# A first activation sum on VectorE, and an output projection with the norms' gains folded into its weights

## The chip, the cores and the metric

The kernel runs on one core of a Trainium2 chip. The metric is the device time of one execution in microseconds (us), as the median of several runs. TensorE (PE) multiplies, VectorE (DVE), ScalarE (ACT) and GpSimd (POOL) work elementwise, and each engine executes its own list of instructions strictly in the order in which the program gave them. Transfers are started by SyncE (SP) and by ScalarE.

## The reference

One layer of a streaming encoder runs over 2048 prompt frames and 64 decode frames, all in float32. D_MODEL is 1024 and D_FF is 2816.

```python
def _merge(attn_o, cmlp_o, norm_attn_g, norm_cmlp_g, w_out):
    cat = jnp.concatenate([_rmsnorm(attn_o, norm_attn_g), _rmsnorm(cmlp_o, norm_cmlp_g)], -1)
    return cat @ w_out

def _post(x, mix, ln1_g, ln1_b, w_gate_up, w_down, ln2_g, ln2_b):
    h = _layernorm(ALPHA * x + mix, ln1_g, ln1_b)
    gu = h @ w_gate_up
    f = (jax.nn.silu(gu[..., :D_FF]) * gu[..., D_FF:]) @ w_down
    return _layernorm(ALPHA * h + f, ln2_g, ln2_b)
```

Ahead of `_merge` stand an input projection, a windowed attention and a gated mixer, which the change does not touch. `_rmsnorm` multiplies each of the 1024 features with a gain of its own, after a scale per row.

## The kernel before

**Exact products from two halves.** A float32 matrix product is made of three fast ones. Each operand is split into hi (ScalarE rounds it to a shorter type) and lo (what is left: source minus hi), and `mm3` adds hi·hi, hi·lo and lo·hi in one PSUM bank. The function `split` does both steps: ScalarE's copy at L112, then the subtraction at L113, on VectorE unless GpSimd is named.

**Output projection and first layer norm (`m2_...`).** The 2112 rows lie in 17 tiles of 128 (tile 16 has 64), taken in the order TSEQ (tiles 0 to 3, 16, then 4 to 15). In what follows a tile's number is its place in TSEQ. A tile passes through these steps:

- `m2_load` brings the concatenated mixers (features by rows, `cat_d`) and the residual x into one buffer `catx`.
- `m2_split` multiplies each of the eight feature blocks by its gain column (`vecT`) and splits it: eight ScalarE instructions (L618) and eight on VectorE (L619) write `cathl`.
- `m2_mm` multiplies with half n of the output columns: 24 matmuls into two PSUM banks `po`, one for the attention features and one for the mixer's.
- `m2_add` scales the residual by ALPHA on ScalarE (L633), adds the attention's bank times its row scale (L634) and then the mixer's bank (L635), both on VectorE.
- `m2_ln` takes mean and variance with `bn_stats` and `bn_aggr` (L642, L644), the inverse root on GpSimd (L92), the gain (L648) and the shift (L649).
- `m2_T` transposes on TensorE (L677), copies to SBUF on ScalarE (L679), and ScalarE issues the stores to `h_d` (L683) and `hy_d` (L684).

A loop over t writes these steps out in a fixed order. For t from 5 to 11 it is: add tile t, multiply tile t+1, norm tile t, split tile t+2, transpose tile t-1, load tile t+3; from t = 6 on a few steps follow that prepare the next stage (`hf`). In that steady part the buffers go round so that `cathl` of tile t+2 lies where `catx` of tile t-2 was, so its first write waits for that tile's store to `hy_d`. The six PSUM banks of the ring "x" hold `po`: the second half of a tile's product needs the banks that the first half of the preceding tile's `m2_add` gives back.

**Feed-forward.** The rows are in four blocks b. Products with the gate and up weights are made by Strassen's scheme, seven `product`s per group i of 128 hidden columns. For blocks 1 to 3 the down projection is Strassen's too, over pairs c of two groups (`strassen`). There are 23 such pairs. From the activations g of a pair, four sums (5, 7, 6 and 3) are made by `f_sums` on GpSimd (L879). `put_hi` (ScalarE, L886) and `put_lo` (VectorE, L890) split a sum, and `unit` multiplies a form's half with its weights (three matmuls, L1333 to L1335) and adds the result to y (L1338). All of this is tied to places p0+q in the list `order` of products. p0 is the place of the pair's last product, whose activation completes the pair. Form 5 is put at p0+3 (hi) and p0+4 (lo), and its first unit stands at p0+5.

Of the kernel before, what the change touches and what calls it, by code (L numbers as in the profile page):

```python
# [8 lines left out]
F32 = mybir.dt.float32  # L9
# [36 lines left out]
def hybrid_step(ctx: ExitStack, tc: tile.TileContext, x_prompt, x_sample, xT_prompt, xT_sample, cache_kT, cache_v, w_in,  # L46
# [541 lines left out]
    def split_wo(hf, n, js):  # L588
        if js[0] == 0:
            wo_hl[hf, n] = [wp.tile([P, 4, 512], F32R, name=f"wo{hf}{n}{s}", tag="W") for s in "hl"]  # L590
        hi, lo = wo_hl[hf, n]
        for j in js:
            split(hi[:, j], lo[:, j], wo_raw.pop((hf, n, j)), nc.gpsimd if j > 1 else None)
            wo[n, 4 * hf + j] = (hi[:, j], lo[:, j])

    cat_t, xr_t, po_t = {}, {}, {}

    def of_f1(name, dt, prod):

# [9 lines left out]
    def m2_split(t, ks=range(KD)):  # L609
        m = rows(t)  # L610
        s = cat_t[t][:, 0].rearrange("p (k q) -> p k q", q=P)
        if ks[0] == 0:
            xr_t[t] = (of_f1("cathl", F32R, 2).rearrange("p (s k q) -> p s k q", s=2, q=P) if t == 3 else
                       wp.tile([P, 2, KD, P], F32R, name="cathl", tag="W"))
        c = xr_t[t]
        for k in ks:
            gcol = vecT[:, 8 + k:9 + k]
            nc.scalar.activation(c[:, 0, k, :m], s[:, k, :m], AF.Copy, scale=gcol)  # L618
            nc.vector.scalar_tensor_tensor(out=c[:, 1, k, :m], in0=s[:, k, :m], scalar=gcol,  # L619
                                           in1=c[:, 0, k, :m].bitcast(F32), op0=ALU.mult, op1=ALU.subtract)  # L620

    def m2_mm(t, n):
        m = rows(t)
# [5 lines left out]
    def m2_add(t, n):  # L629
        m = rows(t)  # L630
        ts_ = cat_t[t][:m, 1, n * 512:(n + 1) * 512]
        po = po_t.pop((t, n))
        nc.scalar.activation(ts_, ts_, AF.Copy, scale=ALPHA)  # L633
        nc.vector.scalar_tensor_tensor(out=ts_, in0=po[0][:m], scalar=rstd_a[:m, t:t + 1], in1=ts_, op0=ALU.mult, op1=ALU.add)  # L634
        nc.vector.tensor_tensor(out=ts_, in0=po[1][:m], in1=ts_, op=ALU.add)  # L635

    def m2_ln(t):
        m = rows(t)
        tt = cat_t[t][:, 1]
        st = const.tile([P, 2, 6], F32, name="hst", tag="hst", bufs=2)  # L640
        for n in range(2):
            nc.vector.bn_stats(st[:m, n], tt[:m, n * 512:(n + 1) * 512])  # L642
        mv = const.tile([P, 2], F32, name="hmv", tag="hmv", bufs=2)
        nc.vector.bn_aggr(mv[:m], st[:m])  # L644
        rs = const.tile([P, 1], F32, name="hrs", tag="hrs", bufs=2)
        rstd(rs[:m], mv[:m, 1:2], m, const)

        nc.vector.scalar_tensor_tensor(out=tt[:m], in0=tt[:m], scalar=mv[:m, 0:1], in1=gb_t[0][:m], op0=ALU.subtract, op1=ALU.mult)  # L648
        nc.vector.scalar_tensor_tensor(out=tt[:m], in0=tt[:m], scalar=rs[:m], in1=gb_t[1][:m], op0=ALU.mult, op1=ALU.add)  # L649

    gb_t = {}
# [219 lines left out]
        f = ffs[b, c, prod] = half_form()  # L871
        split(f[:, 0], f[:, 1], src)

    def f_sums(b, c):

        x, y = g_t.pop((b, 2 * c)), g_t.pop((b, 2 * c + 1))
        for prod, o, a, d, op in ((5, y[:, 1], x[:, 1], y[:, 1], ALU.add), (7, x[:, 1], x[:, 0], x[:, 1], ALU.subtract),
                                  (6, x[:, 0], y[:, 1], x[:, 0], ALU.subtract), (3, y[:, 0], y[:, 0], x[:, 0], ALU.subtract)):
            nc.gpsimd.tensor_tensor(out=o, in0=a, in1=d, op=op)  # L879
        for prod, o in ((5, y[:, 1]), (6, x[:, 0]), (7, x[:, 1]), (3, y[:, 0])):  # L880
            f_sum[b, c, prod] = o

    def put_hi(b, c, prod):

# [12 lines left out]
    def product(b, i, prod):  # L897
        n = TB[b] // 2
        w, h = wf.pop((b, i, prod)), forms[b, prod]
        bk = {1: "A", 6: "A", 7: "A", 4: "A", 2: "B", 5: "C", 3: "C"}[prod]  # L900
        new = prod in (1, 2, 5)
        if new:
            acc[i, bk] = (bank({"A": f"A{i % 2}", "C": f"C{i % 2}", "B": "S1"}[bk]) if b else
                          ps1.tile([P, 512], F32, name=f"acc{bk}", tag="x", bufs=6))
        ps = acc[i, bk][:, :n]
        for k in range(4):
            wh, wl, hh, hl = w[:, 0, k], w[:, 1, k], h[:, 0, k, :n], h[:, 1, k, :n]

            nc.tensor.matmul(ps, wh, hh, start=(new and k == 0), stop=False, skip_group_check=not new)  # L909
            nc.tensor.matmul(ps, wh, hl, start=False, stop=False, skip_group_check=not new)  # L910
            nc.tensor.matmul(ps, wl, hh, start=False, stop=(k == 3), skip_group_check=not new)  # L911

        def keep(key):
            part[i, key] = tmp(key)
            nc.scalar.copy(part[i, key][:, :n], ps)  # L915

        def add(key, to):
            part[i, key] = a = part.pop((i, to))
            nc.vector.tensor_tensor(out=a[:, :n], in0=ps, in1=a[:, :n], op=ALU.add)  # L919

        def out(sh, g, u):
            if strassen(b, i):
                if sh == 0:
                    g_t[b, i] = f2.tile([P, 4, P], F32, name="g", tag="wsum", bufs=3).rearrange("p (s a) q -> p s (a q)", s=2)
                to = g_t[b, i][:, sh]
                nc.vector.tensor_tensor(out=to, in0=u, in1=g, op=ALU.mult)

                if not (sh and i % 2 == 0):
                    put_f(b, i // 2, 4 if sh else 1 + i % 2, to)
                if sh and i % 2:  # L930
                    f_sums(b, i // 2)
                return
            nc.vector.tensor_tensor(out=g, in0=u, in1=g, op=ALU.mult)
            f = ff[b, i][:, :, sh * n:(sh + 1) * n] if b == 0 else half_form()
            if b:
                ff[b, i, sh] = f
            split(f[:, 0], f[:, 1], g)

        if prod == 1:
            keep("a0")  # L940
        elif prod == 6:
            keep("a1")
        elif prod == 7:
            keep("a2")
            part[i, "c22"] = a = part.pop((i, "a2"))
            nc.vector.tensor_tensor(out=a[:, :n], in0=acc[i, "C"][:, :n], in1=a[:, :n], op=ALU.add)
        elif prod == 2:
            add("c11", "a0")
            g = part[i, "c11"][:, :n]
            nc.scalar.activation(g, g, AF.Silu)  # L950
        elif prod == 4:
            if b == 0:
                ff[b, i] = f2.tile([P, 4 * NHX], F32R, name="ff", tag="ff", bufs=4)[:, :4 * n].rearrange("p (s t) -> p s t", s=2)
            out(0, part.pop((i, "c11"))[:, :n], ps)
        elif prod == 3:
            add("c12", "a1")
            g = part.pop((i, "c12"))[:, :n]
            nc.scalar.activation(g, g, AF.Silu)  # L958
            out(1, g, part.pop((i, "c22"))[:, :n])
# [218 lines left out]
    for t in range(NT - 4):  # L1178
        if t == 2 or t > 3:
            m2_add(TSEQ[t + (t == 2)], 0)  # L1180
            m2_add(TSEQ[t + (t == 2)], 1)
        if t == 0 or 3 < t < NT - 5:
            e = 3 if t == 0 else t + 1
            m2_mm(TSEQ[e], 0)
            m2_mm(TSEQ[e], 1)
        m2_ln(TSEQ[t])
        if t == 0 or t > 3:
            m2_split(TSEQ[t + 2 if t else 4])
        if t:
            m2_T(TSEQ[t - 1])  # L1190
        if 0 < t < 4 or 4 < t < NT - 5:
            m2_load(TSEQ[t + 3 if t > 4 else t + 4])
        if t in (1, 2):
            m2_mm(TSEQ[4], t - 1)
        if t == 1:
            m2_split(TSEQ[5])
        if t == 4:

            nc.scalar.activation(warm, neg_half, AF.Silu)
        if t == 6:  # L1200
            prep = [f for _, f in sorted(prep_steps(0), key=lambda e: e[0])]
        if t >= 6:
            for _ in range(4):
                prep.pop(0)()
        if t in (NT - 10, NT - 7):
            load_gu(0, (t - NT + 10) // 3)
# [4 lines left out]
    m2_T(TSEQ[12])  # L1211
    m2_mm(TSEQ[13], 0)
    m2_add(TSEQ[13], 0)
    m2_ln(TSEQ[13])
    m2_load(TSEQ[15])
    m2_split(TSEQ[15])
    sums(0, 0)
# [3 lines left out]
    m2_split(TSEQ[16])  # L1221
    m2_add(TSEQ[14], 1)
    m2_add(TSEQ[14], 0)
    m2_ln(TSEQ[14])
    m2_mm(TSEQ[15], 0)
    m2_T(TSEQ[13])
    m2_add(TSEQ[15], 0)
    make(2)
    m2_mm(TSEQ[15], 1)
    m2_add(TSEQ[15], 1)  # L1230
    m2_ln(TSEQ[15])
    make(3)
    m2_mm(TSEQ[16], 0)
    make(EARLY - 1)
# [1 line left out]
    m2_add(TSEQ[16], 0)  # L1236
    m2_mm(TSEQ[16], 1)
    m2_add(TSEQ[16], 1)
    m2_ln(TSEQ[16])
    store_forms(0)  # L1240
    product(*order[0])
    m2_T(TSEQ[15])
# [210 lines left out]
    for b in range(NB):  # L1453
        first, last = b * NO, b == NB - 1
        for c in range(NFF // 2):
            p0 = start[b, 2 * c + 1, 3]
            d_load, d_split = (-8, -1, -5, -3), (-3, 5, -1, 4)
            if strassen(b, 2 * c):
# [4 lines left out]
                for q, prod, u in ((0, 1, 0), (1, 2, 0), (2, 1, 1), (3, 2, 1), (5, 5, 0), (6, 6, 0), (7, 5, 1), (8, 3, 0), (8, 6, 1),  # L1463
                                   (9, 3, 1), (10, 7, 0), (11, 7, 1), (12, 4, 0), (13, 4, 1)):
                    at(p0 + q, lambda b=b, c=c, prod=prod, u=u: unit(b, c, prod, u))
                for q, prod in ((3, 5), (4, 6), (5, 3), (6, 7)):
                    at(p0 + q, lambda b=b, c=c, prod=prod: put_hi(b, c, prod))
                    at(p0 + q + 1, lambda b=b, c=c, prod=prod: put_lo(b, c, prod))
                continue
# [144 lines left out]
```

## Time and profile before

| | us |
|---|---|
| median of 3 runs (2204.99 to 2209.4) | 2208.36 |
| the profiled execution's own time | 2207.18 |
| its span in the trace | 2205.4 |
| TensorE busy | 2089.7 (95%) |
| VectorE busy | 1640.3 (74%) |
| ScalarE busy | 997.0 (45%) |
| GpSimd busy | 702.2 (32%) |

Busy means that an instruction of the engine was executing. The profiled execution spends 1.8 us outside of its span. The profile gives TensorE's granted clock as a mean of 0.987 of full speed.

### The profile page before, as it was taken

To read this page: it belongs to the slowest core of one execution; us is meant where nothing else is said; L and a number is where in the kernel's file an instruction comes from. 1 tells how busy PE (TensorE), PEld (TensorE's weight loads), DVE (VectorE), ACT (ScalarE), POOL (GpSimd) and SP (SyncE) were. 2 spreads that over 40 slices of the span, in tenths; PEclk is the share of its full clock that TensorE was granted. 3 is DMA by queue.
4 is the path that set the end of the run, shared out by engine and by line. 5 is a ranking of instruction groups with operands and counts; after the bars stand their busy time and mean duration, and the time that the engine had idled before them with its cause. 6 is when DMAs were issued, how large, how long until landed. Compare 5 with 4: busy or idle time off the path is not lost.

```text
span 2205.4 us, 36220 instructions
## 1 busy us (share of the span) xinstructions
PE 2089.7 (95%) x13081; PEld 1861.6 (84%) x13081; DVE 1640.3 (74%) x3176; ACT 997.0 (45%) x2385; POOL 702.2 (32%) x644
## 2 busy tenths in 40 slices
PE   8999999989989899999999999999999999999997
PEld 6888888867768799999888888888888888988986
DVE  6877777786788677777786776777677778577775
ACT  6666666563343444444433443453343444344443
POOL 0222222231132567666531332222243222122221
PEclk9999999989999999999999999999999999999999
DMA  5111111043554866676776767787587777767663
GB/s 196 39 39 39 39 39 39 27 159 118 196 193 172 306 231 235 247 285 241 273 278 240 257 238 277 264 285 278 199 287 273 251 257 276 257 225 262 242 230 121
DMA packets 189156, 447.22 MB, mean 203 GB/s; under 512 B 22608, under 2 KB 53072, under 8 KB 188976
## 3 DMA queue, kind: packets, MB, share of 16 engines
q1 hardware_dynamic: 168432, 426.22, 54.9%
q10 hardware_dynamic: 20368, 18.35, 2.5%
q8 instruction: 103, 1.69, 0.3%
q14 instruction: 77, 0.63, 0.1%
q0 software_dynamic: 176, 0.33, 0.0%
HBM read 345.94 MB, written 98.89 MB: 202 GB/s over the span
## 4 chain that ended last, share of the span: by engine, by line
PE 65%; DVE 20%; ACT 6%; DMA 4%; issue 3%; POOL 1%; ACTq 0%; SPq 0%; DVEq 0%; POOLq 0%
PE bankA L909 5%; PE bankA L911 4%; PE bankA L910 4%; PE pj L158 2%; PE pj L159 2%; PE pj L160 2%; PE bankC L910 2%; PE bankC L909 2%; PE bankC L911 2%; PE pd L159 2%; PE pd L160 2%; PE pd L158 2%; PE bankD L1334 2%; PE bankD L1333 2%; PE bankD L1335 2%
## 5 line engine op out<-in xcount | busy, mean ns | idle before, releaser
L113 POOL TENSOR_TENSOR wf<-guraw,wf 128x512 fp32r<-128x512 f32 x173 | 245.7, 1420 | 626.9 <-ACT wf L112 598.4
L909 PE MATMUL bankA<-hf,wf 128*128 128x256 f32 x1056 | 301.8, 286 | 12.2 <-ACT a L915 11.9
L910 PE MATMUL bankA<-hf,wf 128*128 128x256 f32 x1056 | 300.1, 284 | 0.0
L911 PE MATMUL bankA<-hf,wf 128*128 128x256 f32 x1056 | 299.9, 284 | 0.0
L909 PEld LDWEIGHTS bankA<-hf,wf 128*128 128x128 f32 x1056 | 201.4, 191 | 22.7 <-ACT a L915 14.6
L910 PEld LDWEIGHTS bankA<-hf,wf 128*128 128x128 f32 x1056 | 201.2, 191 | 9.1
L911 PEld LDWEIGHTS bankA<-hf,wf 128*128 128x128 f32 x1056 | 201.4, 191 | 0.0
L112 ACT CAST wf<-guraw 128x512 fp32r<-128x512 f32 x264 | 163.1, 618 | 19.7 <-DMA guraw<-in_w_gate_up_dram 12.6
L915 ACT COPY a<-bankA 128x256 f32<-128x256 f32 x198 | 73.5, 371 | 174.8 <-PE bankA L911 174.4
L910 PE MATMUL bankC<-hf,wf 128*128 128x256 f32 x528 | 149.4, 283 | 2.6 <-DVE hf L113 2.6
L909 PE MATMUL bankC<-hf,wf 128*128 128x256 f32 x528 | 149.8, 284 | 0.9 <-DMA wf<-wf_d 0.8
L911 PE MATMUL bankC<-hf,wf 128*128 128x256 f32 x528 | 148.5, 281 | 0.0
L1338 DVE TENSOR_TENSOR y<-bankD,y 128x512 f32<-128x512 f32 x184 | 125.6, 683 | 30.5 <-PE bankD L1335 30.5
L1326 DVE TENSOR_TENSOR wd<-draw,wd 128x512 fp32r<-128x512 f32 x161 | 130.8, 813 | 0.0
L950 ACT ACTIVATE a<-a 128x256 f32<-128x256 f32 (+1 forms) x88 | 37.4, 425 | 200.7 <-DVE a L919 199.7
L909 PE MATMUL accA<-hf,wf 128*128 128x288 f32 x352 | 105.2, 299 | 8.9 <-ACT a L915 5.3
L958 ACT ACTIVATE a<-a 128x256 f32<-128x256 f32 (+1 forms) x88 | 37.4, 424 | 155.9 <-DVE a L919 155.8
L910 PEld LDWEIGHTS bankC<-hf,wf 128*128 128x128 f32 x528 | 99.5, 188 | 8.6 <-DVE hf L113 3.2
L1338 DVE TENSOR_TENSOR y<-bankS,y 128x512 f32<-128x512 f32 x138 | 94.4, 684 | 16.1 <-PE bankS L1335 13.7
L909 PEld LDWEIGHTS bankC<-hf,wf 128*128 128x128 f32 x528 | 99.8, 189 | 7.0 <-DMA wf<-wf_d 1.4
L911 PE MATMUL accA<-hf,wf 128*128 128x288 f32 x352 | 104.1, 296 | 0.4 <-DVE wf L113 0.4
L910 PE MATMUL accA<-hf,wf 128*128 128x288 f32 x352 | 104.4, 297 | 0.0
(336 smaller groups left out, 6712.1 us busy)
## 6 DMA issues: line engine op xcount, KB each, us to landing
wf<-wf_d SPq DMA_DIRECT2D x264, 512.0 KB, 4.9
guraw<-in_w_gate_up_dram SPq DMA_DIRECT2D x110, 512.0 KB, 6.2
wf_d<-wf SPq DMA_DIRECT2D x88, 512.0 KB, 4.9
draw<-in_w_down_dram SPq DMA_DIRECT2D x153, 256.0 KB, 3.5
draw<-wt_d SPq DMA_DIRECT2D x92, 256.0 KB, 4.3
guraw<-in_w_gate_up_dram SPq DMA_DIRECT2D x66, 256.0 KB, 6.4
wt_d<-draw SPq DMA_DIRECT2D x44, 256.0 KB, 3.3
hraw<-h_d SPq DMA_DIRECT2D x42, 256.0 KB, 4.7
```

Of the source, the lines that this page charges most:

```text
L112: nc.scalar.copy(hi, src)
L113: (on or nc.vector).tensor_tensor(out=lo, in0=src, in1=hi.bitcast(F32), op=ALU.subtract)
L158: nc.tensor.matmul(out, ah, bh, start=(i == 0), stop=False)
L159: nc.tensor.matmul(out, ah, bl, start=False, stop=False)
L160: nc.tensor.matmul(out, al, bh, start=False, stop=(i == n - 1))
L909: nc.tensor.matmul(ps, wh, hh, start=(new and k == 0), stop=False, skip_group_check=not new)
L910: nc.tensor.matmul(ps, wh, hl, start=False, stop=False, skip_group_check=not new)
L911: nc.tensor.matmul(ps, wl, hh, start=False, stop=(k == 3), skip_group_check=not new)
L915: nc.scalar.copy(part[i, key][:, :n], ps)
L1326: nc.vector.tensor_tensor(out=hl[:, 1], in0=d_raw.pop((b, c, "f", prod)), in1=hl[:, 0].bitcast(F32), op=ALU.subtract)
L1333: nc.tensor.matmul(pd, fh, w[:, 0], start=new, stop=False, skip_group_check=not new)
L1338: nc.vector.tensor_tensor(out=y, in0=pd, in1=y, op=ALU.add)
```

## The change

Two places change, and each is independent of the other.

**In the projection.** The gains move from the activations into the weights, once, in `split_wo`, so `m2_split` becomes a plain `split` of the whole tile: one ScalarE and one VectorE instruction of 1024 columns (two of 512 for the first three tiles). ALPHA moves into a VectorE addition that takes the mixer's bank first, and the second addition writes the row sums as well (`accum_out`). `bn_stats` and `bn_aggr` go. ScalarE squares the centred row and sums it, and `m2_ln` is cut in two at a `yield`: where the loop splits tile t+2, that split now stands between the two parts of tile t's norm.

**In the feed-forward.** The sum for form 5 is made by VectorE right after the product that completes the pair, in a buffer that is free by then; GpSimd makes the other three. `put_hi` and `put_lo` of form 5 stand one place earlier.

```diff
     def split_wo(hf, n, js):
...
         for j in js:
-            split(hi[:, j], lo[:, j], wo_raw.pop((hf, n, j)), nc.gpsimd if j > 1 else None)
+            raw, gcol = wo_raw.pop((hf, n, j)), vecT[:, 8 + 4 * hf + j:9 + 4 * hf + j]
+            if j > 1:
+                nc.scalar.activation(raw, raw, AF.Copy, scale=gcol)
+                split(hi[:, j], lo[:, j], raw, nc.gpsimd)
+            else:
+                nc.scalar.activation(hi[:, j], raw, AF.Copy, scale=gcol)
+                nc.vector.scalar_tensor_tensor(out=lo[:, j], in0=raw, scalar=gcol, in1=hi[:, j].bitcast(F32), op0=ALU.mult, op1=ALU.subtract)
...
     def m2_split(t, ks=range(KD)):
...
-        for k in ks:
-            gcol = vecT[:, 8 + k:9 + k]
-            nc.scalar.activation(c[:, 0, k, :m], s[:, k, :m], AF.Copy, scale=gcol)
-            nc.vector.scalar_tensor_tensor(out=c[:, 1, k, :m], in0=s[:, k, :m], scalar=gcol,
-                                           in1=c[:, 0, k, :m].bitcast(F32), op0=ALU.mult, op1=ALU.subtract)
+        ks = slice(ks[0], ks[-1] + 1)
+        split(c[:, 0, ks, :m], c[:, 1, ks, :m], s[:, ks, :m])
...
     def m2_add(t, n):
...
-        nc.scalar.activation(ts_, ts_, AF.Copy, scale=ALPHA)
-        nc.vector.scalar_tensor_tensor(out=ts_, in0=po[0][:m], scalar=rstd_a[:m, t:t + 1], in1=ts_, op0=ALU.mult, op1=ALU.add)
-        nc.vector.tensor_tensor(out=ts_, in0=po[1][:m], in1=ts_, op=ALU.add)
+        nc.vector.scalar_tensor_tensor(out=ts_, in0=ts_, scalar=ALPHA, in1=po[1][:m], op0=ALU.mult, op1=ALU.add)
+        nc.vector.scalar_tensor_tensor(out=ts_, in0=po[0][:m], scalar=rstd_a[:m, t:t + 1], in1=ts_, op0=ALU.mult, op1=ALU.add,
+                                       accum_out=hsum[t][:m, n:n + 1])
...
     def m2_ln(t):
...
+        nc.vector.tensor_scalar(hs[:m, 2:3], hs[:m, 0:1], hs[:m, 1:2], -1.0 / D, op0=ALU.add, op1=ALU.mult)
+        nc.scalar.activation(cat_t[t][:m, 0], tt[:m], AF.Square, bias=hs[:m, 2:3],
+                             accum_out=hs[:m, 3:4])
+        yield
+        nc.vector.tensor_scalar(hs[:m, 3:4], hs[:m, 3:4], 1.0 / D, None, op0=ALU.mult)
         rs = const.tile([P, 1], F32, name="hrs", tag="hrs", bufs=2)
...
-    def f_sums(b, c):
+    def f_sums(b, c, first):
...
+        for prod, o, a, d in ((7, x[:, 1], x[:, 0], x[:, 1]), (6, x[:, 0], first, x[:, 0]), (3, y[:, 0], y[:, 0], x[:, 0])):
+            nc.gpsimd.tensor_tensor(out=o, in0=a, in1=d, op=ALU.subtract)
             f_sum[b, c, prod] = o
+        f_sum[b, c, 5] = first
...
                 nc.vector.tensor_tensor(out=to, in0=u, in1=g, op=ALU.mult)
+                if sh and i % 2:
+                    nc.vector.tensor_tensor(out=u, in0=g_t[b, i - 1][:, 1], in1=to, op=ALU.add)
...
-        m2_ln(TSEQ[t])
+        go(m2_ln, TSEQ[t])
         if t == 0 or t > 3:
             m2_split(TSEQ[t + 2 if t else 4])
+        go(m2_ln, TSEQ[t])
...
-                for q, prod in ((3, 5), (4, 6), (5, 3), (6, 7)):
+                for q, prod in ((2, 5), (4, 6), (5, 3), (6, 7)):
```

The first place is VectorE in the feed-forward, from the additions around the product at p0+3 of a pair to the first unit of form 6. `ff<-g` at L890 is `put_lo`, `wd` a weight's lo half, `y<-bank` a unit's result, and the lines with `bankS` and `bankC` add up a product. Before:

```order
L919 TENSOR_TENSOR a_18217<-bankS_12228,a_18217 128x256
L1326 TENSOR_TENSOR wd<-draw,wd 128x512
L1338 TENSOR_TENSOR y<-bankS_12902,y 128x512
L946 TENSOR_TENSOR a_18374<-bankC_12168,a_18374 128x256
L1326 TENSOR_TENSOR wd<-draw,wd 128x512
L890 TENSOR_TENSOR ff<-g,ff 128x256
```

With the change, where two rows of the product at p0 stand ahead, then a line of "...", then the same place (lines have moved by some 7 to 15):

```order
L933 TENSOR_TENSOR g_17967<-a2_17918,a1_17865 128x256
L936 TENSOR_TENSOR a2_17918<-g_17782,g_17967 128x256
...
L926 TENSOR_TENSOR a0_17942<-bankS1_11953,a0_17942 128x256
L1341 TENSOR_TENSOR wd_18047<-draw_17951,wd_18047 128x512
L1353 TENSOR_TENSOR y_16354<-bankS0_12627,y_16354 128x512
L897 TENSOR_TENSOR ff_18053<-a2_17918,ff_18053 128x256
L956 TENSOR_TENSOR a2_18100<-bankC0_11893,a2_18100 128x256
```

The sum (L936) is new, and `put_lo` of form 5 (now L897) has moved ahead of the addition to the next product (now L956) and of the lo half of a later weight.

The second place is VectorE in the projection, one turn of the loop (tile t = 8). `po` are the four PSUM banks, `cathl` at L619 and L113 is the split of tile t+2, and `hf` prepares the next stage. Before:

```order
L634 SCALAR_TENSOR_TENSOR catx<-po_6970,rstd_a,catx 128x512
L635 TENSOR_TENSOR catx<-po_6971,catx 128x512
L634 SCALAR_TENSOR_TENSOR catx<-po_6996,rstd_a,catx 128x512
L635 TENSOR_TENSOR catx<-po_6997,catx 128x512
L642 BN_STATS hst<-catx 128x6 x2
L644 BN_AGGR hmv<-hst 128x2
L91 TENSOR_SCALAR rs_e<-hmv 128x1
L648 SCALAR_TENSOR_TENSOR catx<-catx,hmv,gb 128x1024
L649 SCALAR_TENSOR_TENSOR catx<-catx,hrs,gb 128x1024
L619 SCALAR_TENSOR_TENSOR cathl<-catx,vecT,cathl 128x128 x8
```

With the change:

```order
L639 SCALAR_TENSOR_TENSOR catx<-catx,po_6820 128x512
L640 SCALAR_TENSOR_TENSOR catx,hsum<-po_6819,rstd_a,catx 128x512
L639 SCALAR_TENSOR_TENSOR catx<-catx,po_6846 128x512
L640 SCALAR_TENSOR_TENSOR catx,hsum<-po_6845,rstd_a,catx 128x512
L647 TENSOR_SCALAR hsum<-hsum 128x1
L113 TENSOR_TENSOR cathl<-catx,cathl 128x1024
L652 TENSOR_SCALAR hsum<-hsum 128x1
L91 TENSOR_SCALAR rs_e<-hsum 128x1
L656 SCALAR_TENSOR_TENSOR catx<-catx,hsum,gb 128x1024
L657 SCALAR_TENSOR_TENSOR catx<-catx,hrs,gb 128x1024
```

The split of tile t+2 stood behind tile t's gain and shift and now stands ahead of them.

The third place is ScalarE in the projection, two turns of the same loop. Before:

```order
L618 ACTIVATE cathl<-catx,vecT 128x128 x8
L679 ACTIVATE catx<-hTp 128x512 x2
L683 DMA h_d_88<-catx 1024x1x128
L684 DMA hy_d_95<-catx 128x1024
L633 ACTIVATE catx<-catx 128x512 x2
L618 ACTIVATE cathl<-catx,vecT 128x128 x8
```

With the change:

```order
L112 CAST cathl<-catx 128x1024
L687 ACTIVATE catx<-hTp 128x512 x2
L691 DMA h_d_88<-catx 1024x1x128
L692 DMA hy_d_95<-catx 128x1024
L649 ACTIVATE catx,hsum<-catx,hsum 128x1024
L112 CAST cathl<-catx 128x1024
```

The scaling by ALPHA is gone, the square (L649) is new ahead of the split, and the split is one instruction.

## Rows read from the trace of the kernel before

**Rows 1.** The page's first line.

```profile
span 2205.4 us, 36220 instructions
```

**Rows 2.** Windows: projection alone, then the feed-forward's blocks 1 to 3.

```profile
core 0: us, PE busy (x) PEld busy (x) DVE busy (x) ACT busy (x) POOL busy (x), PEclk, DMA share, GB/s
...
517.00:715.00 198.00, 180.83 (x848) 145.02 (x849) 165.96 (x292) 79.75 (x197) 47.87 (x31) 0.97 0.53 179
...
1190.00:2150.00 960.00, 916.33 (x6283) 842.76 (x6282) 700.87 (x1187) 386.76 (x879) 265.04 (x234) 0.99 0.73 254
```

**Rows 3.** The line of put_lo: duration ns min/median/max, and who waited (us, times).

```profile
L890 DVE TENSOR_TENSOR ff<-g,ff x92: 408/418/1502, 1224.4 to 2138.1; 128x256 fp32r<-128x256 f32 x92
...
  PE bankS L1335: 25.3, 23
```

**Rows 4.** Timeline of TensorE: start, us, what; in brackets idle before, releaser.

```profile
1737.81 0.40 PE L1333 MATMUL bankD<-wd,ff 128*128 128x512 f32 x1
...
1738.51 0.28 PE L909 MATMUL bankS<-hf,wf 128*128 128x256 f32 x1
...
1743.48 0.39 PE L1333 MATMUL bankS<-wd,ff 128*128 128x512 f32 x1
1745.16 0.50 PE L1335 MATMUL bankS<-wd,ff 128*128 128x512 f32 x1 [1.05 <-DVE ff L890]
1745.50 0.28 PE L909 MATMUL bankA<-hf,wf 128*128 128x256 f32 x1
...
1747.41 0.40 PE L1335 MATMUL bankD<-wd,ff 128*128 128x512 f32 x1
```

**Rows 5.** Timeline of the other engines around the same unit of one pair.

```profile
1741.13 0.68 DVE L1338 TENSOR_TENSOR y<-bankS,y 128x512 f32<-128x512 f32 x1
...
1743.00 0.68 DVE L1326 TENSOR_TENSOR wd<-draw,wd 128x512 fp32r<-128x512 f32 x1
...
1743.53 1.29 POOL L113 TENSOR_TENSOR wf<-guraw,wf 128x512 fp32r<-128x512 f32 x1 [2.87 <-ACT wf L112]
1743.60 1.50 DVE L890 TENSOR_TENSOR ff<-g,ff 128x256 fp32r<-128x256 f32 x1
...
1746.31 0.42 DVE L890 TENSOR_TENSOR ff<-g,ff 128x256 fp32r<-128x256 f32 x1
```

**Rows 6.** Groups in 517 to 715 us: count, busy us, mean ns, idle before.

```profile
L619 DVE SCALAR_TENSOR_TENSOR cathl<-catx,vecT,cathl 128x128 fp32r<-128x128 f32 (+1 forms) x112 | 36.9, 394 | 11.5 <-ACT cathl L618 11.4
L618 ACT ACTIVATE cathl<-catx,vecT 128x128 fp32r<-128x128 f32 (+1 forms) x112 | 33.9, 386 | 54.3 <-DMA hy_d<-catx 49.1 <-PE po L160 5.2
L649 DVE SCALAR_TENSOR_TENSOR catx<-catx,hrs,gb 128x1024 f32<-128x1024 f32 (+1 forms) x17 | 28.4, 1673 | 7.5 <-POOL hrs L92 7.5
...
L642 DVE BATCH_NORM_STATS2 hst<-catx 128x6 f32<-128x512 f32 (+1 forms) x34 | 21.7, 681 | 0.1
L648 DVE SCALAR_TENSOR_TENSOR catx<-catx,hmv,gb 128x1024 f32<-128x1024 f32 (+1 forms) x17 | 21.7, 1275 | 0.0
L635 DVE TENSOR_TENSOR catx<-po,catx 128x512 f32<-128x512 f32 (+1 forms) x30 | 20.7, 691 | 4.5 <-PE po L160 1.9
```

**Rows 7.** Timeline of TensorE in the projection: three of its waits.

```profile
517.29 0.47 PE L158 MATMUL po<-wo00h,cathl 128*128 128x512 f32 x1 [1.07 <-issue]
...
623.54 0.50 PE L160 MATMUL po<-wo00h,cathl 128*128 128x512 f32 x1 [1.78 <-DVE cathl L619]
...
662.22 1.94 PE L677 MATMUL hTp<-ident,catx 128*128 128x128 f32 x8 [5.49 <-ACT catx L679]
```

**Rows 8.** Timeline of ScalarE around a store to hy_d and the split behind it.

```profile
650.12 0.62 ACTq L684 DMA_DIRECT2D hy_d<-catx  x1
...
658.68 2.45 ACT L618 ACTIVATE cathl<-catx,vecT 128x128 fp32r<-128x128 f32 x8 [5.60 <-DMA hy_d<-catx]
661.03 1.05 ACT L679 ACTIVATE catx<-hTp 128x512 f32<-128x512 f32 x2
```

**Rows 9.** The store to hy_d at its line: us to landing.

```profile
DMA to landing us min/median/max: 3.2/5.1/10.3
```

More of the change, by code (lines that the diff above doesn't have):

```diff
@@ L592, in split_wo @@
         for j in js:
-            split(hi[:, j], lo[:, j], wo_raw.pop((hf, n, j)), nc.gpsimd if j > 1 else None)
+            raw, gcol = wo_raw.pop((hf, n, j)), vecT[:, 8 + 4 * hf + j:9 + 4 * hf + j]
[5 more added lines that the diff above has]
+                nc.vector.scalar_tensor_tensor(out=lo[:, j], in0=raw, scalar=gcol, in1=hi[:, j].bitcast(F32), op0=ALU.mult, op1=ALU.subtract)
             wo[n, 4 * hf + j] = (hi[:, j], lo[:, j])
-    cat_t, xr_t, po_t = {}, {}, {}
+    cat_t, xr_t, po_t, hsum = {}, {}, {}, {}
     def of_f1(name, dt, prod):
@@ L632, in m2_add @@
         po = po_t.pop((t, n))
-        nc.scalar.activation(ts_, ts_, AF.Copy, scale=ALPHA)
-        nc.vector.scalar_tensor_tensor(out=ts_, in0=po[0][:m], scalar=rstd_a[:m, t:t + 1], in1=ts_, op0=ALU.mult, op1=ALU.add)
-        nc.vector.tensor_tensor(out=ts_, in0=po[1][:m], in1=ts_, op=ALU.add)
+        if t not in hsum:
+            hsum[t] = const.tile([P, 4], F32, name="hsum", tag="hsums", bufs=3)
+        nc.vector.scalar_tensor_tensor(out=ts_, in0=ts_, scalar=ALPHA, in1=po[1][:m], op0=ALU.mult, op1=ALU.add)
+        nc.vector.scalar_tensor_tensor(out=ts_, in0=po[0][:m], scalar=rstd_a[:m, t:t + 1], in1=ts_, op0=ALU.mult, op1=ALU.add,
+                                       accum_out=hsum[t][:m, n:n + 1])
     def m2_ln(t):
@@ L639, in m2_ln @@
         tt = cat_t[t][:, 1]
[L640 to L644, printed above, removed]
+        hs = hsum.pop(t)
+        nc.vector.tensor_scalar(hs[:m, 2:3], hs[:m, 0:1], hs[:m, 1:2], -1.0 / D, op0=ALU.add, op1=ALU.mult)
[3 more added lines that the diff above has]
+        nc.vector.tensor_scalar(hs[:m, 3:4], hs[:m, 3:4], 1.0 / D, None, op0=ALU.mult)
         rs = const.tile([P, 1], F32, name="hrs", tag="hrs", bufs=2)
-        rstd(rs[:m], mv[:m, 1:2], m, const)
-        nc.vector.scalar_tensor_tensor(out=tt[:m], in0=tt[:m], scalar=mv[:m, 0:1], in1=gb_t[0][:m], op0=ALU.subtract, op1=ALU.mult)
+        rstd(rs[:m], hs[:m, 3:4], m, const)
+        nc.vector.scalar_tensor_tensor(out=tt[:m], in0=tt[:m], scalar=hs[:m, 2:3], in1=gb_t[0][:m], op0=ALU.add, op1=ALU.mult)
         nc.vector.scalar_tensor_tensor(out=tt[:m], in0=tt[:m], scalar=rs[:m], in1=gb_t[1][:m], op0=ALU.mult, op1=ALU.add)
@@ L872, in put_f @@
         split(f[:, 0], f[:, 1], src)
-    def f_sums(b, c):
+    def f_sums(b, c, first):
         x, y = g_t.pop((b, 2 * c)), g_t.pop((b, 2 * c + 1))
[L877 to L880, printed above, removed]
+        for prod, o, a, d in ((7, x[:, 1], x[:, 0], x[:, 1]), (6, x[:, 0], first, x[:, 0]), (3, y[:, 0], y[:, 0], x[:, 0])):
+            nc.gpsimd.tensor_tensor(out=o, in0=a, in1=d, op=ALU.subtract)
             f_sum[b, c, prod] = o
+        f_sum[b, c, 5] = first
     def put_hi(b, c, prod):
@@ L930, in out @@
                 if sh and i % 2:
-                    f_sums(b, i // 2)
+                    f_sums(b, i // 2, u)
                 return
@@ L1213, in hybrid_step @@
     m2_add(TSEQ[13], 0)
-    m2_ln(TSEQ[13])
+    go(m2_ln, TSEQ[13])
+    go(m2_ln, TSEQ[13])
     m2_load(TSEQ[15])
@@ L1223, in hybrid_step @@
     m2_add(TSEQ[14], 0)
-    m2_ln(TSEQ[14])
+    go(m2_ln, TSEQ[14])
+    go(m2_ln, TSEQ[14])
     m2_mm(TSEQ[15], 0)
@@ L1230, in hybrid_step @@
     m2_add(TSEQ[15], 1)
-    m2_ln(TSEQ[15])
+    go(m2_ln, TSEQ[15])
+    go(m2_ln, TSEQ[15])
     make(3)
@@ L1238, in hybrid_step @@
     m2_add(TSEQ[16], 1)
-    m2_ln(TSEQ[16])
+    go(m2_ln, TSEQ[16])
+    go(m2_ln, TSEQ[16])
     store_forms(0)
```

## The prediction, made before the change was run

> **What bounds the kernel now.** I read the busy shares first: TensorE is busy 95% of the span [rows 1], so a change pays only where TensorE itself waits, or if it makes TensorE wait. The windows then show where it has room [rows 2]. In the feed-forward's blocks 1 to 3 it is idle 960.00 − 916.33 = 43.7 us, and in the projection 198.00 − 180.83 = 17.2 us. These two sums are the ceilings of what the two halves of the change can return, apart from some clock: it is granted at 0.97 in the projection and 0.99 in the feed-forward, both near the upper level of 2.4 GHz.
>
> Next, who ends those waits. Of the feed-forward's 43.7 us, 25.3 us stand on one line: the first matmul that reads lo of a sum waits for `put_lo`, 23 times [rows 3], which is once in each of the 23 pairs. The timeline of one pair shows the place [rows 4]: the unit's first matmul (L1333, hi) runs at 1743.48, and the third (L1335, lo) starts at 1745.16 after 1.05 idle. The other engines show why lo is late [rows 5]. VectorE runs its list in order. `put_lo` of form 5 stands behind the lo half of a weight (1743.00, 0.68), which stands behind the addition to the next product. It then runs from 1743.60 for 1.50 us, where the next one (1746.31) takes 0.42; a GpSimd subtraction has been running since 1743.53 for 1.29. So it is late by its place and slow by its neighbour.
>
> The projection has no such single line. Its groups [rows 6] show VectorE at 166 of 198 us [rows 2], with the eight-fold split (L619, 36.9 us), `bn_stats` (21.7), gain (21.7) and shift (28.4). TensorE's waits there are of several kinds [rows 7]: 1.07 for the first split, 1.78 for a lo, and once 5.49 for ScalarE's copies of a transpose, which stood behind a split that waited for a store [rows 8].
>
> **The feed-forward, part by part.** *What a wait costs.* With the wait, from L1333 to the next product's first matmul takes 1745.50 − 1743.48 = 2.02 us; where nothing is waited for, 1738.51 − 1737.81 = 0.70 [rows 4]. The loss is 1.32, of which 1.05 is the idle time and 0.27 the restart. Over the trace: 25.3 + 23 × 0.27 = 31.5 us.
>
> *Does the wait go?* After the change `put_lo` of form 5 stands directly behind the addition of the unit before it, L1338, which runs from 1741.13 for 0.68 to 1741.81 [rows 5]. Its source no longer comes from GpSimd, and its hi is made a place earlier by ScalarE, which is busy 387 of 960 us [rows 2]. So lo is ready at 1741.81 + 0.42 = 1742.2, or at 1743.3 if it is again slowed to 1.50. TensorE began to wait for it at 1745.16 − 1.05 = 1744.1 [rows 4]. Both ends are ahead of that, by 0.8 to 1.9 us. I take the whole 31.5.
>
> *The sum moved to VectorE.* It costs 23 times 0.42 (the 128x256 operation [rows 5]) to 1.50 (beside GpSimd), 9.7 to 34.5 us on an engine that idles 960 − 701 = 259 us there [rows 2]. Its cover is that: what stands right behind it, the lo of form 4, has its unit only at p0+12. The buffer is a product's working tile, which is not written again for several places. GpSimd loses 23 additions and keeps the rest, with 265 of 960 us busy. I price this at 0.
>
> *What is late next?* `put_lo` of form 6: at present it ends at 1746.73 [rows 5], and the matmul on bank D that reads it starts at 1747.41 [rows 4], 0.7 us of slack. With 1.32 us taken out ahead of it, TensorE arrives earlier, but VectorE also sheds 1.5 us ahead of that row, so the order stays. If a GpSimd subtraction meets it, it would take up to 1.1 us more and a wait of 0.4 us would show. For the range: −25 (only the idle time returns) to −33 (waits of other lines shrink a little too).
>
> The Trainium skill, "SBUF — State Buffer", section "Who interferes with whom", says that a VectorE instruction with two SBUF inputs shares a port with GpSimd's reads, and that the first to hold it keeps it for its whole instruction. The trace agrees: 1.50 against 0.42 [rows 5]. The rule speaks against the change, which adds 23 such instructions: by it each could be held back 1.1 us, 25 us on VectorE; by the place of the rows these lie where nothing waits.
>
> **The projection, part by part.** *Work per tile.* VectorE: the split goes from 8 × 0.394 = 3.15 (its mean [rows 6]; this includes slowed ones) to one 128x1024 subtraction, which I price as the gain at 1.28; `bn_stats` 2 × 0.68 goes for two tiny operations of perhaps 0.15; the row sum in the addition is not in this trace: between 0 and 0.7 (another pass as long as L642), I take 0.2 for each of two. Together VectorE loses about 2.5 us a tile. ScalarE: the split goes from 2.45 to about 1.05 (two copies of 512 take 1.05 [rows 8]), the two scalings by ALPHA go, and a square of 1024 of about 1.2 comes. Nothing of this is on TensorE's path by itself; eight more ScalarE scalings of raw weights, once, are covered by the loads ahead of the stage.
>
> *Gains.* What is relieved is the wait at 623.54 with its neighbours (some 3.5 us: VectorE behind with lo) and small ones like it, about 2 us. The ceiling is the 17.2 idle; I bound the gain by 11, since the 5.49 at 662.22 is of another kind.
>
> *Losses.* First, the first tiles' splits are in one piece: TensorE needs the whole hi and lo (1.05 + 1.28) instead of the first eighths (0.386 + 0.394), 1.5 us where it waits for them, as at 517.29 [rows 7]. Second, a new wait. Gain and shift of tile t now stand on VectorE behind lo of tile t+2. Its hi waits for the store of tile t−2, which lands 3.2 to 10.3 us after its issue, 5.1 at the median [rows 9]; 8.56 in rows 8 (650.12 to 658.68). Behind it queue the gain, the inverse root (GpSimd, 7.5/17 = 0.44 [rows 6]), the shift, and then the next tile's additions, for which TensorE's banks wait. One turn: copies and issue 1.4, landing L, hi 1.05, lo 1.28, small ones 0.3, gain 1.28, root 0.44, shift 1.28 to 1.67, additions 4 × 0.68 (as L1338 [rows 5]) and the row sums, 3.1: 10.1 to 10.5 + L. TensorE asks for the first additions' banks about 16 us after the transposes of tile t−2 (tile t+1 at 198/17 = 11.65, a transpose of 1.94 [rows 7], and some of the next tile's first half), and only 1.5 of the 3.1 are needed by then. So it stalls where L is above about 7.5, a few tiles, and by 1 to 3 us each. At 662.22 the transposes that now wait for copies until 662.1 wait for gain and shift as well: hi 658.68 to 659.73, lo 661.0, then 0.3 + 1.28 + 0.44 + 1.28 gives 664.3, some 2 us later. Together +6.5: 1.5, 2 and about 3 for two tiles with a late store.
>
> *Net.* +6.5 − 5.5 = +1 us, with −11 and +9 as ends.
>
> **Sum.** −31.5 + 1.0 = −30.5. The profiled execution took 2207.18, 1.8 outside of its span, which stays; it lies 1.2 below the median of 2208.36. 2207.2 − 30.5 = 2176.7, and I say 2177.
>
> **The rivals.** *The projection's relief wins.* VectorE's 166 us are what TensorE's 17.2 idle come from, and 2.5 us a tile is more than any of its usual waits: −11 instead of +1, about 2165. Against it: a third of the idle time is behind ScalarE and the store, which stay.
>
> *Half the feed-forward wait comes back.* Form 6's lo, or the earlier `put_lo` beside GpSimd work that also moves earlier, is late by 0.7 us in each of 23 pairs: 16 us, about 2193. For it: the slack is 0.8 to 1.9 for form 5 and 0.7 for form 6, a GpSimd meeting costs 1.1. Against it: GpSimd is busy 28% of the time, so it should meet a few pairs, not all.
>
> *The change doesn't do what it says in the feed-forward.* The lo would still be last, because hi on ScalarE or the place itself is late: 2208. Against it: the sum is made at p0, two places ahead of the hi, and the lo's old hindrances stand behind it now.
>
> *Slower.* VectorE gets stuck behind the store in every turn of the loop. To eat the 31 us and 4.4 more, the fourteen turns must lose 2.5 us each, so by the 7.5 above, the store must land after about 10 us every time: 2212 or more. For it: 8.56 and 10.3 were seen. Against: the median is 5.1.
>
> **How the numbers follow.** Forecast 0.67 (2168 to 2186); relief in the projection 0.13; half of the wait back 0.12; no effect in the feed-forward 0.03; slower 0.05. A measurement of this kernel tells about 0.2%, 4.4 us, from no change. Faster takes the first three, 0.92; the same 0.03; slower 0.05. The range takes in the relief whole and most of the half wait: 2165 to 2192, which leaves out about 0.15.
>
> **What would show it.** Right: no wait of the lo matmul (now L1350) for `put_lo` of form 5, and the period of a pair shorter by 1.3; the sum (L936) at 0.4 to 1.5 with VectorE's idle time smaller and no TensorE wait on it; in the projection VectorE's busy time down by about 40 us with TensorE's idle time near 17, and the transposes of tile 12 later. Wrong: waits on form 6's lo; TensorE waiting for a `po` bank in many turns, with VectorE idle in front of the split's subtraction (L113) by more than 5 us each; a row sum that doubles the additions.

## The result, and the profile after

The median is 2178.2 us of 4 runs (2175.85 to 2182.78) against 2208.5 of 4 runs before, 30.3 us less. The means are 29.1 apart, a ratio of 0.9868 with a 95% interval of 0.9847 to 0.989. The profiled execution took 2175.85.

The page's busy times come first, then windows with the columns of [rows 2]: the projection between the same instructions as there, and the feed-forward from the first `unit` of the 23 pairs to the last. The third window is that feed-forward stretch in the kernel before.

```profile
PE 2082.8 (96%) x13081; PEld 1857.4 (85%) x13081; DVE 1584.2 (73%) x3100; ACT 982.9 (45%) x2277; POOL 690.5 (32%) x621
```

```profile
520.00:724.00 204.00, 183.69 (x848) 147.50 (x849) 129.18 (x207) 63.90 (x103) 48.80 (x31) 0.96 0.51 173
1224.80:2117.60 892.80, 872.29 (x6112) 807.41 (x6111) 670.05 (x1188) 379.45 (x862) 250.38 (x208) 0.99 0.77 268
```

```profile
1214.50:2148.50 934.00, 890.33 (x6113) 818.96 (x6112) 687.66 (x1165) 379.06 (x862) 261.14 (x231) 0.99 0.73 256
```

The same 848 matmuls of the projection take 204 us where they took 198, although VectorE has 37 us less to do there. The feed-forward stretch is 41.2 us shorter, more than the 31.5 of the forecast, and only 23 of it is idle time: TensorE's busy time fell by 18.0 with the same matmuls.

What became of the 23 waits shows on `put_lo`'s line (now L897; columns as in [rows 3]), where form 5 reads the tile `a`:

```profile
L897 DVE TENSOR_TENSOR ff<-a,ff x23: 408/417/921, 1232.6 to 2097.2; 128x256 fp32r<-128x256 f32 x23
...
  PE bankD L1350: 0.5, 2
```

and in the timelines of TensorE and of VectorE at the place of [rows 4, 5]:

```profile
1730.07 0.40 PE L1348 MATMUL bankS<-wd,ff 128*128 128x512 f32 x1
...
1730.54 0.39 PE L1350 MATMUL bankS<-wd,ff 128*128 128x512 f32 x1
1730.78 0.28 PE L916 MATMUL bankA<-hf,wf 128*128 128x256 f32 x1
```

```profile
1727.72 0.68 DVE L1353 TENSOR_TENSOR y<-bankS,y 128x512 f32<-128x512 f32 x1
1728.32 0.41 DVE L897 TENSOR_TENSOR ff<-a,ff 128x256 fp32r<-128x256 f32 x1
```

From L1348 to the next product it is 0.71 us, the unwaited distance; lo is there at 1728.73, 1.8 ahead of L1350. Set against each other matmul by matmul, the two timelines differ by 31.7 us at these 23 places together. Another 9.5 comes off in steps of some 2 ns on the mean, nearly all at matmuls that wait for nothing.

In the projection, TensorE's longest new waits, and what stands ahead of them on VectorE and on ScalarE:

```profile
520.53 0.47 PE L158 MATMUL po<-wo00h,cathl 128*128 128x512 f32 x1 [1.72 <-issue]
521.79 0.50 PE L160 MATMUL po<-wo00h,cathl 128*128 128x512 f32 x1 [0.56 <-DVE cathl L113]
...
612.14 0.50 PE L158 MATMUL po<-wo01h,cathl 128*128 128x512 f32 x1 [2.22 <-DVE catx L639]
...
658.51 1.41 PE L685 MATMUL hTp<-ident,catx 128*128 128x128 f32 x8 [3.69 <-DVE catx L657]
```

```profile
652.84 1.23 DVE L113 TENSOR_TENSOR cathl<-catx,cathl 128x1024 fp32r<-128x1024 f32 x1 [2.25 <-ACT cathl L112]
...
655.95 2.42 DVE L657 SCALAR_TENSOR_TENSOR catx<-catx,hrs,gb 128x1024 f32<-128x1024 f32 x1 [0.44 <-POOL hrs L92]
```

```profile
602.28 1.04 ACT L112 CAST cathl<-catx 128x1024 fp32r<-128x1024 f32 x1 [7.83 <-DMA hy_d<-catx]
...
650.62 1.15 ACT L649 ACTIVATE catx<-catx,hsum 128x1024 f32<-128x1024 f32 x1 [4.05 <-DVE hsum L647]
...
651.77 1.03 ACT L112 CAST cathl<-catx 128x1024 fp32r<-128x1024 f32 x1
```

Both late places have VectorE idle for the split's hi; then lo, gain and shift (beside GpSimd 2.42) run one after the other. But the hi is late for different reasons. At 602.28 ScalarE has waited 7.83 for the store, as the prediction has it, and the additions behind come late for TensorE's bank: 2.22 (before: 0.91). At 651.77 it has not waited for a store. The hi starts straight behind the square (L649), and the square had to wait for the row sums of the additions (4.05). VectorE idles 2.25 meanwhile, and the transposes wait 3.69 (before: 1.42). The same pause of 2.25 stands in four turns.

Behind the first wait, at 520.53, the clock fell; the window over the 5.5 us from 520.5:

```profile
520.50:526.00 5.50, 4.92 (x13) 3.60 (x14) 4.07 (x8) 1.31 (x3) 0.00 (x0) 0.69 0.28 112
```

### The profile page after: what moved, and what is told of

Read it like the earlier page. It is cut to its first block, busy times and chain, and to the rows that moved or that the text cites. A ratio compares the mean times of both kernels' runs of the same rounds, so it can differ in the third digit from the quotient of the medians.

```text
span 2174.1 us, 35972 instructions
## 1 busy us (share of the span) xinstructions
PE 2082.8 (96%) x13081; PEld 1857.4 (85%) x13081; DVE 1584.2 (73%) x3100; ACT 982.9 (45%) x2277; POOL 690.5 (32%) x621
## 4 chain that ended last, share of the span: by engine, by line
PE 68%; DVE 18%; DMA 5%; ACT 5%; issue 3%; POOL 1%; ACTq 0%; SPq 0%; DVEq 0%; POOLq 0%
PE bankA L916 5%; PE bankA L917 5%; PE bankA L918 5%; PE pj L158 2%; PE bankC L917 2%; PE pj L159 2%; PE bankC L916 2%; PE pj L160 2%; PE bankC L918 2%; PE pd L159 2%; PE pd L160 2%; PE pd L158 2%; PE po L160 2%; PE po L158 2%; PE accA L918 2%
## 5 line engine op out<-in xcount | busy, mean ns | idle before, releaser
L113 POOL TENSOR_TENSOR wf<-guraw,wf 128x512 fp32r<-128x512 f32 x173 | 246.0, 1422 | 608.4 <-ACT wf L112 573.7
L916 PE MATMUL bankA<-hf,wf 128*128 128x256 f32 x1056 | 298.6, 283 | 12.7 <-ACT a L922 12.6
L917 PE MATMUL bankA<-hf,wf 128*128 128x256 f32 x1056 | 296.7, 281 | 0.0
L918 PE MATMUL bankA<-hf,wf 128*128 128x256 f32 x1056 | 296.6, 281 | 0.0
L918 PEld LDWEIGHTS bankA<-hf,wf 128*128 128x128 f32 x1056 | 200.6, 190 | 0.0
```

Of the source, the lines that this page charges most:

```text
L113: (on or nc.vector).tensor_tensor(out=lo, in0=src, in1=hi.bitcast(F32), op=ALU.subtract)
```

## The experiments

Three numbers of each run's trace stand beside its time: the projection's length (from the start of the last eight transposes of the gains to that of the last eight of a tile), whether the 23 waits are there, and the pace, the mean distance between the starts of neighbouring unwaited 128x256 matmuls in blocks 1 to 3 (about 4,000 in each run). Place is where the forms hf lie, which these matmuls read as their moving operand (the one with the 256 columns): their address in bytes in the built program, modulo 128. The versions have 2 to 10 runs each.

| run | median us | ratio to before, 95% | projection us | 23 waits | place | pace ns |
|---|---|---|---|---|---|---|
| before | 2207.4 to 2208.6 | | 198.4 | yes | 0 | 118.9 |
| the change | 2178.2 | 0.9847 to 0.989 | 204.8 | no | 32 | 117.1 |
| e1_ff | 2180.5 | 0.9853 to 0.9895 | 199.6 | no | 0 | 118.8 |
| e2_proj | 2209.6 | 0.9988 to 1.0012 | 203.9 | yes | 32 | 117.2 |
| e3_norm_first | 2177.1 | 0.9844 to 0.9879 | 202.3 | no | 32 | 117.2 |
| e4_split_halves | 2176.1 | 0.983 to 0.9873 | 201.3 | no | 32 | 117.1 |
| e5_undo_shift | 2185.8 | 0.9887 to 0.9916 | 204.6 | no | 0 | 118.8 |
| e6_ff_shift | 2174.3 | 0.9836 to 0.9869 | 198.8 | no | 32 | 117.1 |
| e7_sum_gpsimd | 2176.5 | 0.9839 to 0.9878 | 202.7 | no | 32 | 117.0 |
| e8_old_place | 2205.7 | 0.9978 to 0.9998 | 204.3 | yes | 32 | 117.1 |
| e9_both | 2171.1 | 0.982 to 0.9854 | 197.2 | no | 32 | 117.0 |
| e10_forms_64 | 2172.6 | 0.9815 to 0.9862 | 198.5 | no | 64 | 117.7 |
| e11_forms_96 | 2180.2 | 0.985 to 0.9896 | 200.6 | no | 96 | 119.9 |
| e12_forms_apart | 2178.3 | 0.983 to 0.9906 | 198.1 | no | 32 and 0 | mixed |

**The halves apart.** e1_ff is the kernel before with the three feed-forward hunks of the diff, e2_proj with the others.

> Only the feed-forward half of the change, on the kernel before. Theory A (from aligning the two traces: the 23 waits return 31.7 us, the projection half costs 8 to 10, and the feed-forward's matmuls also run 9.5 us shorter in sum, because of this half): 2167 us, and the 9.5 is seen again in the trace. Theory B (that pace belongs to the run, not to the change): 2176, or the 9.5 comes and goes between runs. The rival that the projection half costs nothing, as predicted: 2177, like the full change.

> Only the projection half of the change, on the kernel before. Theory A: slower, 2216 to 2219 us, with TensorE's losses of the full change at the same places: the start of the stage after the gains' transposes, the wait for the additions near 600, and the transposes that wait for the shift near 650. The rival (the prediction's sum, +1): 2207 to 2210.

The feed-forward half alone is worth 27.7 us. Its 2180.5 is not theory A's 2167; the 2176 and the 2177 of the others lie within the spread of its runs, 4 us to either side. Its matmuls keep the pace of before, 118.8 ns. The projection half alone changes nothing in the time, as the prediction's +1 had it. But its trace has the losses of the full change (203.9 us in the projection), and its untouched feed-forward runs at 117.2 ns. So the 9.5 us goes with the projection half, and theory A had it at the wrong half.

**Two repairs of the projection.** e3_norm_first:

```diff
         go(m2_ln, TSEQ[t])
+        go(m2_ln, TSEQ[t])
         if t == 0 or t > 3:
             m2_split(TSEQ[t + 2 if t else 4])
-        go(m2_ln, TSEQ[t])
```

> The full change, but the second part of the norm (variance, gain, shift) stands ahead of the split of tile t+2 again. Theory A (most of the projection half's loss comes from gain and shift behind the split that waits for the store): 4 to 7 us faster than the full change, about 2172, and the waits for the shift near 650 and for the additions near 600 fall back to 1.4 and 0.9 us or less. The rival (the loss comes from the split in one piece and from the clock after a wait): within 1.5 us of 2178. A second rival: VectorE now waits 1.5 us for ScalarE's square in every turn, and the additions come late: 2185.

e4_split_halves:

```diff
-        ks = slice(ks[0], ks[-1] + 1)
-        split(c[:, 0, ks, :m], c[:, 1, ks, :m], s[:, ks, :m])
+        for k0 in range(ks[0], ks[-1] + 1, 4):
+            kq = slice(k0, k0 + 4)
+            split(c[:, 0, kq, :m], c[:, 1, kq, :m], s[:, kq, :m])
```

> The full change, but every split of the projection is made in two halves of four blocks each (two ScalarE and two VectorE instructions of 512 columns for one of 1024 each). If the loss at the start of the stage (a wait of 0.56 for lo, and a clock of 0.69 for the 5.5 us behind it) and the two later waits of 0.4 to 1.1 for hi and 0.5 for lo come from the split in one piece: 3 to 4 us faster than the full change, 2174 to 2175. If these come from elsewhere: 2178 to 2179.

The medians, 1 and 2 us below the change, lie within the spread of the runs; the traces tell more. With the norm first, the wait at 612 is gone and the transposes near 650 wait 1.62, as the row of e3_norm_first shows, but lo of a later tile, now behind the norm, makes TensorE wait again, once 2.94:

```profile
632.06 0.55 PE L160 MATMUL po<-wo00h,cathl 128*128 128x512 f32 x1 [2.94 <-DVE cathl L113]
...
658.97 1.06 PE L685 MATMUL hTp<-ident,catx 128*128 128x128 f32 x8 [1.62 <-DVE catx L657]
```

That is the wait at 623.54 [rows 7] come back: the change's order had removed it, and paid for it near 600 and 650. The square stays ahead of the hi on ScalarE in this run; the other order was not tried. With the halves, the wait for lo at the start is gone and the clock holds, in the window of e4_split_halves over 5.5 us at the same place:

```profile
521.00:526.50 5.50, 5.32 (x22) 4.04 (x23) 4.13 (x9) 1.69 (x4) 0.00 (x0) 1.00 0.38 142
```

e9_both has both edits.

> The full change with both repairs of the projection: the second part of the norm ahead of the split of tile t+2, and every split in two halves. From the traces of the two apart (halves return 2.5 us between the gains' transposes and the first transpose of a tile, the norm's order 2.5 us between the first and the last transpose): 5 us below the full change, 2173, as fast as the feed-forward half with the forms at the new place (2174). If the two returns share one cause: 2176.

In the traces the two returns add up, and a little more: the projection takes 197.2 us, 7.6 less than with the change. The median is 7.1 below the change's and the lowest here, but its interval still overlaps those of most versions without the 23 waits, e6_ff_shift with the old projection among them.

**Where the pace comes from.** The names of the buffers and their addresses in the built programs gave the theory: the change drops `hst` and `hmv` and adds `hsum`, and all that is allocated behind them moves down by 96 bytes. e5_undo_shift:

```diff
     vecT = const.tile([P, 32], F32, name="vecT")
+    const.tile([P, 24], F32, name="pad2")
```

> The full change, and 96 unused bytes in the pool of constants. The projection half removes two small tiles and adds another, so that every buffer behind them, the forms hf among them that the feed-forward's matmuls read, lies 96 bytes lower than before; the unused bytes put them back. Theory D (the pace of the 256-column matmuls, 118.8 ns apart in the two runs with the old places and 117.1 to 117.2 in the four with the new, is set by where the forms lie): the pace returns to 118.8, and the time is 12 us above the full change, about 2190. The rival (the pace comes from the order of work on the other engines, or from the run): 2178 and 117.1.

e6_ff_shift, on e1_ff:

```diff
-    const.tile([P, 24], F32, name="pad")
```

> Only the feed-forward half of the change on the kernel before, without the 96 unused bytes that its pool of constants has at its start, so that the forms lie where the full change has them; the projection is that of the kernel before. Theory D: pace 117.1 ns, 12 us below the feed-forward half alone, 2168. By the same theory the projection half then costs about 10 us as the difference to the full change's 2178. The rival: 2180, as the feed-forward half alone.

Both paces came as theory D said. The times moved by 7.6 and 6.2, not by 12. The intervals of each two versions just overlap, so the pace shows the effect more surely than the time. An estimate from the paces: 1.7 ns for each of the 5,544 matmuls of 128x256 are 9.4 us. The 1,848 of 128x288 in block 0 became slower by 0.7 ns, which takes 1.3 back: some 8 us. At equal places the projection half costs 5.3 (e5_undo_shift against e1_ff) and 3.9 (the change against e6_ff_shift). e10_forms_64 and e11_forms_96 replace the 24 of that line by 8 and by 16:

> Only the feed-forward half on the kernel before, with 32 unused bytes instead of 96: the forms lie at 64 bytes past a multiple of 128 (before: 0, with the change: 32). If the pace of the 256-column matmuls goes by the place within 64 bytes: 118.8 ns and 2180. If any place other than a multiple of 128 is good: 117.1 and 2172.

> The same with 64 unused bytes: the forms lie at 96 bytes past a multiple of 128. If the pace goes by the place within 64 bytes: 117.1 ns and 2172, as at 32. If 32 is a place of its own: 118.8 and 2180.

Neither rule holds: four places, four paces (118.8, 117.1, 117.7, 119.9). e12_forms_apart, on e6_ff_shift, moves four of the seven forms back:

```diff
     m2_split(TSEQ[3])
+    f1.tile([P, 24], F32, name="apart")
```

> The feed-forward half with the forms moved, and 96 unused bytes between them: forms 2, 3 and 4 lie at 32 bytes past a multiple of 128, forms 1, 5, 6 and 7 (and the raw tiles between them) at a multiple of 128. If the pace is that of the form which a matmul reads: a product of form 2 to 4 runs at 117.1 ns for each 256-column matmul and one of form 1, 5, 6 or 7 at 118.8, in the same run; bank S (form 2) is faster than banks A and C. If it comes from another buffer that moves along: one pace for all, and banks S, A and C alike within 0.7 ns. The time: between 2168 and 2180.

The pace is the form's own. First and last matmul of two products of e12_forms_apart in TensorE's timeline, bank S (form 2, not moved back) and bank A:

```profile
1500.48 0.28 PE L907 MATMUL bankS<-hf,wf 128*128 128x256 f32 x1
...
1501.77 0.28 PE L909 MATMUL bankS<-hf,wf 128*128 128x256 f32 x1
...
1503.30 0.28 PE L907 MATMUL bankA<-hf,wf 128*128 128x256 f32 x1
...
1504.61 0.28 PE L909 MATMUL bankA<-hf,wf 128*128 128x256 f32 x1
```

That is 1.29/11 = 117.3 and 1.31/11 = 119.1 ns. Over the run, bank S has 117.1, C 117.8 and A 118.4, the last two being mixtures; in e6_ff_shift they have 117.5, 117.1 and 117.1. Taken apart by the form that each product reads, e12_forms_apart has 117.2, 116.9 and 117.1 for forms 2, 3 and 4, and 119.1, 118.6, 118.7 and 119.0 for forms 1, 5, 6 and 7.

**What took the 23 waits away.** e7_sum_gpsimd leaves the places and gives the sum back to GpSimd:

```diff
-                if sh and i % 2:
-                    nc.vector.tensor_tensor(out=u, in0=g_t[b, i - 1][:, 1], in1=to, op=ALU.add)
...
+        nc.gpsimd.tensor_tensor(out=first, in0=x[:, 1], in1=y[:, 1], op=ALU.add)
         for prod, o, a, d in ((7, x[:, 1], x[:, 0], x[:, 1]), (6, x[:, 0], first, x[:, 0]), (3, y[:, 0], y[:, 0], x[:, 0])):
```

> The full change, but the sum for form 5 stays on GpSimd, as the first of its four, and put_hi and put_lo keep their earlier places. If the place on VectorE's list is what took the wait away (the prediction's reason): 2178 to 2181, no wait for form 5. If the sum has to be on VectorE because GpSimd is late with it: the wait returns on put_hi, by 0.5 to 1.3 us in each of 23 pairs, 2190 to 2208.

e8_old_place leaves the sum on VectorE:

```diff
-                for q, prod in ((2, 5), (4, 6), (5, 3), (6, 7)):
+                for q, prod in ((3, 5), (4, 6), (5, 3), (6, 7)):
```

> The full change, but put_hi and put_lo of form 5 stand at their old places; the sum is on VectorE. If the place is what counts: 23 waits of about 1.05 again, and 2178 + 31 = 2209. If the slow put_lo beside GpSimd's subtraction was enough of the cause, and GpSimd now runs that earlier: put_lo ends about 1.1 us sooner, and most of the wait is gone, 2180 to 2185.

The first changes nothing, the second gives all 23 waits back. Its line of `put_lo`:

```profile
L897 DVE TENSOR_TENSOR ff<-a,ff x23: 1477/1502/1505, 1235.7 to 2127.2; 128x256 fp32r<-128x256 f32 x23
...
  PE bankS L1350: 25.6, 23
```

At the old place every one of the 23 takes 1.48 to 1.51 us. So the one place earlier is the whole of the feed-forward's gain, and the sum's move is worth nothing that these runs tell. What the runs don't part is the two things that the earlier place does: `put_lo` starts sooner, and it hardly meets GpSimd's subtraction any more (0.42 us at the median, 0.92 at most). An estimate from [rows 4, 5]: at its old start and unslowed, lo would have been there at 1743.60 + 0.42 = 1744.0, just before TensorE began to wait at 1744.1. To move the subtraction instead was not tried.

## Why the prediction was right, and where it was not

**The feed-forward wait: right, in size and cause.** 31.7 us at the 23 places against 31.5, with a slack of 1.8 (0.8 to 1.9 forecast). By times it is 27.7 (e1_ff against before) and 27.5 (the change against e8_old_place), within the spread of the runs. Form 6's lo is waited for twice, 0.5 us in all. That the place is the cause is shown (e7_sum_gpsimd, e8_old_place); how much of it is the start and how much the neighbour is open.

**The sum on VectorE: right.** 23 times 0.425 us (0.424 to 0.427), none slowed, and no matmul waits for it. What the Trainium skill, "SBUF — State Buffer", section "Who interferes with whom", holds against such instructions happened to `put_lo` at its old place, 23 times of 23, and not once to the sum: whether it costs is a matter of place.

**The projection's net of +1: wrong.** The prices held: lo 1.23 (1.28 forecast), additions with row sum 1.5 a pair, VectorE down 37 us (40). The row sum is a read of the accumulator of 0.08 a time (0.2 forecast); the Trainium skill, "VectorE: DVE Perf Modes", section "Two Vector instructions with no wait between them", says that an operation which writes its accumulator out is two instructions, and the trace shows the second. What failed is the sum that was made of them. The numbers that follow come from the two traces set against each other matmul by matmul; the projection is 6.4 us longer in this pair.

- *The one-piece split at the start, put at 1.5, cost 3.3.* The waits are 1.4, as forecast. But TensorE then ran more than half of the 5.5 us behind them at the lower clock, 1.2 GHz (matmuls of 0.63 us instead of 0.40), for which the sum has no term. From the start of the last eight transposes of the gains to that of the first eight of a tile it is 16.4 us against 13.1. At two later tiles, near 566 and 604, waits for the hi and lo of a whole tile cost 2.4 more.
- *The gains, put at 5.5, are about 4.* The wait at 623.54 and its neighbours gave back 3.1. At 662.22, where the forecast had a loss of 2, the wait is 0.9 shorter.
- *The turn with a late store, put at about 3 for two tiles, cost 1.3 at one,* near 600.
- *The turn's sum leaves out the square.* It was priced at 1.2 and held to be off TensorE's path. But on ScalarE it stands ahead of the hi, and it has to wait for the row sums. Near 650 that, and not the store, made hi, lo, gain and shift late: 2.1 us of wait and 1.6 at the lower clock behind it (0.69 granted over the 5.5 us from 658.5, before: 1.00).

Over the traces of all versions the loss is 5.1: the mean over the five with the projection as changed is 204.1, over the six with the old one 199.0.

**A term that was not there: the forms' place.** The prediction's sum has no row for what a removed buffer does to the addresses behind it. That gave back up to 9.5 us in the trace (1.7 ns for each of the 4,860 matmuls of 128x256 in that stretch are 8) and 6 to 8 by the times. The two errors cancel, and that is luck: that the projection half alone measures 1.000 looks like the forecast confirmed, and is a loss of 5 and a gain of about as much at another place. The total, 2178.2 against the 2177 of the forecast, owes its closeness to the same luck.

**The rivals.** None came: the relief did not win, form 6 waits for 0.5 us in all and not for 16, and VectorE behind the store cost a single tile, not every turn.

Open is why a place has its pace: four places were tried, not more, and whether hi or lo of a form decides was not tried. Part of the time between runs of one kernel, some 3 us to either side, has no cause named here.

## What to carry to other kernels

A late operand can be mended by its place in its engine's list; try the move alone before moving the work to another engine. Cutting work on an engine that waits pays nothing if the same edit puts its urgent instructions behind one that waits for a transfer or for another engine's new work, so follow that chain through every engine's list. A split in one piece makes the first matmul wait for all of it, and a wait can cost the lower clock behind it as well. When an edit adds or drops a small buffer, look at the pace of untouched matmuls before you credit the edit: addresses behind it have moved.

## What was not expected of the hardware

The pace of these matmuls depends on where their moving operand starts: for 128x256 in blocks 1 to 3, 118.8 ns at 0, 117.1 at 32, 117.7 at 64 and 119.9 at 96 bytes past a multiple of 128, within 0.2 ns of these in each block of each run with all forms at one place. The order is another for the 128x288 matmuls of block 0: 133.0, 133.7, 132.2 and 132.2.
